# The first loads and the first two head pairs of a tree-masked attention kernel, put in another order

## The chip, the cores and the metric

One core of one Trainium2 chip runs the kernel. The metric is the device time of one execution in microseconds (us); the time before is 132.62 us, the median of three runs (132.22 to 132.91). Engines are named as in the profile: PE is TensorE (PEld its weight loads), DVE VectorE, ACT ScalarE, POOL GpSimd, SP SyncE.

## The reference

Attention over 8 batches of 12 heads (96 heads in all), 512 positions of 64 numbers. A position may see itself and its ancestors in a binary tree, in which the parent of i is (i-1)//2.

```python
for i in range(seq):
    mask[i, i] = 1
    parent = i
    while parent > 0:
        parent = (parent - 1) // 2
        mask[i, parent] = 1
scores = np.einsum('bhqd,bhkd->bhqk', Q, K) * scale
scores = scores + (1 - mask) * (-1e9)
weights = np.exp(scores - np.max(scores, axis=-1, keepdims=True))
weights = weights / (np.sum(weights, axis=-1, keepdims=True) + 1e-10)
return np.einsum('bhqk,bhkd->bhqd', weights, V).astype(np.float32)
```

Inputs and output are float32.

## The kernel before

**Pairs.** The 96 heads are worked on as 48 pairs, `i` from 0 to 47. A pair passes through these steps, each of them a function of the program:

- `transpose(i)` (steps "T", or "K" and "Q" for the two halves alone): TensorE turns K and Q of the pair, so that the 64 numbers lie across partitions, into one PSUM tile `kqp`. There is a single buffer for it (the pool `psT` has one), so the transposes of a pair wait until VectorE has copied those of the pair before.
- `evac(i)`: VectorE copies `kqp` to the SBUF tile `kq` (L459 in the first four pairs).
- `scores1(i)` and `scores2(i)` (step "S"): TensorE multiplies mask codes (L503, L528) and keys and queries (L508, L534) into the PSUM tiles `s1` and `s2`; ScalarE takes the exponentials (L519, L550) into `e`.
- `values(i - 1)` and `norm(i - 1)` (step "V"): TensorE multiplies exponentials and `vt` into `ob` (L561); `vt` is V in the order of the tree, with a column of ones that gives the sums. VectorE takes the reciprocal of the sums (L594) and multiplies (L599).

**V copies.** V is loaded as `vst` and brought into the order of the tree by small copies, `spread` (L309), each named by (block of 16 heads, part 0 to 9, first head, last head). Which engine makes which copy, and behind which pair, is written out in the tables `BY_VECTOR` and `BY_SCALAR`; the rest is GpSimd's. Step "D" issues VectorE's copies of the pair's number, step "A" ScalarE's; where a string has no "D" or "A", they come at its end.

**Order.** Nothing is scheduled by a tool: each engine runs its instructions in the order in which the program issues them. For the first six pairs the order of the steps is a string in the list `FIRST`; later pairs use "STV" and the like. Step "X" is `spin`: two matmuls of zeros on TensorE (L745) that nobody reads. Ahead of the loop stand nine more of these, the cast of the first loads (L758), and the transposes and evacuation of pair 0.

**Loads.** K and Q of heads 0 and 1 come through the queues of SP and ACT into `ol`, as float32. All other loads, and nearly all stores, are issued by GpSimd in one program, the list `ops`, and cast to bf16 on the way; `load_k`, `load_q` and `load_v` take the first head and the number of heads (L260; L270 for the groups from head 8 on). Between the loads stand GpSimd's own copies: `eye_order` and `code_order` (the tiles `mixed`, L243, and `qcoarse`, L248) early on. An operation of `ops` is issued as soon as the pairs are far enough (`ready`), and then runs in the order of the list.

Of the kernel before, what the change touches and what calls it, by code (L numbers as in the profile page):

```python
# [124 lines left out]
def kernel(  # L125
# [495 lines left out]
    def pool_program():  # L621

        K_BEFORE = {
            6: (load_k, 8 * KB, KB), 10: (spread_top, 5, 0, KB), 11: (store, nc.gpsimd, 5),
        }

        Q_BEFORE = {
            3: (load_k, 5 * KB, KB), 4: (load_k, 6 * KB, KB), 5: (spread_top, 3, 0, KB), 6: (spread_top, 3, KB, VB),
            9: (spread_top, 4, KB, VB), 10: (spread_top, 5, KB, VB),
        }  # L630
        ops = [
            (load_k, 2, 2), (load_q, 2, 2), (load_v, 0, 8), (load_k, 4, 4),
            (load_q, 4, 2), (load_q, 6, 2), (load_k, 8, 8), (load_q, 8, 8), (eye_order,),
            (load_v, 8, 8), (code_order, 0), (code_order, 64),
            (load_k, 16, 8), (load_q, 16, 8), (load_v, 16, 8),
            (load_k, 24, 8), (load_q, 24, 8), (load_v, 24, 8),
            (load_k, 32, 8), (spread_top, 0, KB, VB), (spread_top, 1, 0, KB),
            (load_v, 32, 8), (load_q, 32, 8), (load_k, 40, 8),
            (spread_top, 1, KB, VB),
        ]  # L640
        stored = 0
        for h in range(40, NH, KB):
            if h == 40:
                ops += [(load_v, h, KB), (load_q, h, KB)]
            else:
                ops += [(load_k, h, KB), (load_q, h, KB)]
            if h + KB < NH:
                ops.append((load_v, h + KB, KB))
            if h % VB == KB:
                ops.append((spread_top, h // VB, 0, KB))  # L650
            elif h >= 48:
                ops.append((spread_top, h // VB - 1, KB, VB))
            while KB * stored + KB + BEHIND <= h + KB:
                ops.append((store, nc.gpsimd, stored))
                stored += 1
        ops.append((spread_top, NH // VB - 1, KB, VB))
        ops += [(store, nc.gpsimd, q) for q in range(stored, NH // KB - 1)]
        ops += [(store_pair, nc.gpsimd, i) for i in (NP - 4, NP - 3)]
        for g in BESIDE["Q"]:
            if g in Q_BEFORE:  # L660
                ops.insert(ops.index(Q_BEFORE[g]), (lay_q, g))
                continue
            at = ops.index((load_q, KB * g, KB)) + 1
            behind = 0
            while behind < LANES:
                behind += {load_k: 1, load_q: 1, load_v: 1, store: 2, store_pair: 1}.get(ops[at][0], 0)
                at += 1
            ops.insert(at, (lay_q, g))
        for g in K_BY_POOL:
            before = K_BEFORE.get(g, (lay_q, g))  # L670
            ops.insert(ops.index(before), (lay_early, g))
        return ops

    def ready(op, i):
# [16 lines left out]
        return i >= GP * (args[1] + 1)  # L691

    BY_VECTOR = {
# [29 lines left out]
    def spread_by(copy, table, steady, i):  # L723
# [6 lines left out]
        for args in todo:  # L730
            spread(copy, *args)

    program = pool_program()

    def pool(i):
# [22 lines left out]
        nc.vector.tensor_copy(out=kept[0][:, 0:2, :, :], in_=first[src][:, :, :, :])  # L758
    TWICE = (9,)
    K_TURN = {3: 7, 4: 10, 5: 14}  # L760
    FIRST = ['XKSQ', 'SXXXKXQDVAT', 'SVATT', 'SVTT', 'STV', 'STVD']
    done = 1
    pool(-1)
    transpose(0)
# [2 lines left out]
    for i in range(NP + 1):  # L767
        steps = FIRST[i] if i < len(FIRST) else "STVT" if i in TWICE else "SVT" if i == 8 else "STV"
        for n, step in enumerate(steps):
# [67 lines left out]
```

## Time and profile before

| | before |
|---|---|
| time, median of 3 runs | 132.62 us |
| time of the profiled execution | 132.39 us |
| its span | 130.6 us |
| busy: PE, DVE, ACT, POOL | 114.5, 96.8, 97.9, 95.5 us |
| read and written in HBM | 37.86 MB, 12.58 MB |

The span runs from the first to the last recorded event of the execution; the time includes what lies around it. Times within the trace are us from the span's start. A row of the timeline gives start, duration, engine, line of the kernel, operation, output tile <- input tile with their shapes, the number of instructions, and in brackets how long the engine sat idle before and what ended that. A row of the chain of waits gives start, duration and the work that the end depended on at that moment. "To landing" of a load is the time from its issue until its data are there.

### The profile page before, as it was taken

The numbers are of one execution on the slowest core, as the hardware profiler recorded it, in microseconds if no ns is written. First come the engines' busy times: TensorE is split into PE (matmuls) and PEld (weight loads), VectorE is DVE, ScalarE is ACT, GpSimd is POOL, SyncE is SP. The second block draws the span as 40 slices with busy tenths as digits, with TensorE's granted clock in tenths as the row PEclk, the third lists the DMA queues.
The fourth block names the chain that finished last, engine by engine and source line by source line (L and its number), as shares of the span: only waits on it lengthen the run. The fifth ranks groups of instructions, "written<-read, shape, count | busy, mean of one in ns | idle before, by whom it ended". The sixth has DMA issues, their size and how long they took to land.

```text
span 130.6 us, 4946 instructions
## 1 busy us (share of the span) xinstructions
PE 114.5 (88%) x2130; PEld 82.2 (63%) x2131; DVE 96.8 (74%) x185; ACT 97.9 (75%) x160; POOL 95.5 (73%) x147
## 2 busy tenths in 40 slices
PE   4989767899799878699999999999999999989960
PEld 1343545667576656477676777776777768766640
DVE  4529957774996897996996877898958788666560
ACT  4359245797766695868979789789798997898940
POOL 6999546029779899999999999669899999200420
PEclk9999999999999999999999999999999999999995
DMA  2999999999999999999999999999999999999993
GB/s 86 228 185 205 214 198 215 195 211 205 208 201 210 206 208 201 211 203 211 206 207 207 209 347 226 203 336 241 204 311 266 267 382 385 379 388 403 380 355 136
DMA packets 24533, 32.12 MB, mean 246 GB/s; under 512 B 945, under 2 KB 15921, under 8 KB 24513
## 3 DMA queue, kind: packets, MB, share of 16 engines
q0 software_dynamic: 23232, 30.67, 111.0%
q1 hardware_dynamic: 720, 0.70, 1.6%
q10 hardware_dynamic: 560, 0.46, 1.1%
q8 instruction: 16, 0.26, 0.7%
q14 instruction: 5, 0.03, 0.1%
HBM read 37.86 MB, written 12.58 MB: 386 GB/s over the span
## 4 chain that ended last, share of the span: by engine, by line
PE 48%; DVE 25%; ACT 12%; DMA 5%; issue 5%; POOL 1%; ACTq 0%; POOLq 0%
PE ob L561 14%; DVE vt L309 7%; DVE of L599 6%; ACT e L550 6%; PE s L503 6%; PE kqp L384 6%; PE s L528 6%; DVE kq L445 6%; DMA vst<-in_V_dram 5%; PE kqp L406 5%; PE s L534 5%; PE s L508 5%; ACT e L519 4%; DVE kq L453 2%; DVE rec L594 2%
## 5 line engine op out<-in xcount | busy, mean ns | idle before, releaser
L519 ACT ACTIVATE e<-s 128x1024 bf16<-128x1024 f32 x48 | 49.2, 1024 | 23.2 <-PE s L508 22.6
L309 POOL COPY vt<-vst 32x256 uint32<-32x256 uint32 (+2 forms) x70 | 35.9, 512 | 10.7 <-DMA vst<-in_V_dram 7.6
L550 ACT ACTIVATE e<-s 128x384 bf16<-128x384 f32 (+1 forms) x92 | 41.4, 504 | 0.0
L561 PE MATMUL ob<-vt,e 128*128 128x65 bf16 (+1 forms) x940 | 37.3, 197 | 2.5 <-DVE of L599 1.8
L561 PEld LDWEIGHTS <-e 128*128 128x128 bf16 (+1 forms) x960 | 31.4, 102 | 7.8 <-DVE of L599 3.2
L599 DVE TENSOR_TENSOR of<-ob,rec 128x512 f32<-128x512 f32 x44 | 30.4, 692 | 1.5
L309 DVE COPY vt<-vst 32x512 uint32<-32x512 uint32 (+4 forms) x37 | 20.4, 552 | 1.7 <-DMA vst<-in_V_dram 0.7
L534 PEld LDWEIGHTS <-kq 64*128 64x128 bf16 x384 | 16.3, 110 | 6.2
L508 PE MATMUL s<-kq 64*128 64x512 bf16 x96 | 18.4, 378 | 1.3 <-DVE kq L445 1.3
L594 DVE RECIPROCAL rec<-ob 128x8 f32<-128x8 f32 x47 | 9.6, 204 | 13.1 <-PE ob L561 12.9
L453 DVE COPY kq<-kqp 128x1024 bf16<-128x1024 bf16 x22 | 15.1, 688 | 3.9 <-PE kqp L384 3.3
L534 PE MATMUL s<-kq 64*128 64x160 bf16 (+1 forms) x384 | 17.9, 210 | 0.0
L528 PE MATMUL s<-qcoarse,codes 40*128 40x480 bf16 x88 | 16.3, 364 | 1.3 <-ACT e L550 1.1
L503 PE MATMUL s<-qcoarse,codes 40*128 40x512 bf16 x88 | 17.2, 385 | 0.0
L445 DVE COPY kq<-kqp 128x2048 bf16<-128x2048 bf16 x11 | 13.5, 1225 | 5.0 <-PE kqp L406 4.9
L607 POOL DMA_DIRECT2D out_dram<-of x11 | 9.9, 906 | 9.0 <-DVE of L599 9.0
L528 PEld LDWEIGHTS <-codes 40*128 40x128 bf16 x96 | 7.5, 95 | 11.1 <-issue 4.7
L384 PE MATMUL kqp<-mixed,Kbeside 128*128 128x128 bf16 x144 | 11.1, 220 | 1.4 <-DVE Kbeside L333 1.2
L406 PE MATMUL kqp<-ptile,Qbeside 128*128 128x128 bf16 x144 | 11.1, 220 | 0.4 <-DVE kq L453 0.4
L333 POOL COPY Qbeside<-qst 128x1024 uint32<-128x1024 uint32 x9 | 9.5, 1059 | 2.4 <-DMA qst<-in_Q_dram 2.3
L260 POOL DMA_DIRECT2D vst<-in_V_dram x12 | 10.9, 909 | 0.0
L270 POOL DMA_DIRECT2D kst<-in_K_dram x11 | 7.8, 709 | 3.4 <-PE kqp L384 1.8
(45 smaller groups left out, 100.3 us busy)
## 6 DMA issues: line engine op xcount, KB each, us to landing
out_dram<-of POOLq DMA_DIRECT2D x11, 1024.0 KB, 10.2
vst<-in_V_dram POOLq DMA_DIRECT2D x12, 512.0 KB, 14.5
kst<-in_K_dram POOLq DMA_DIRECT2D x11, 512.0 KB, 11.9
qst<-in_Q_dram POOLq DMA_DIRECT2D x11, 512.0 KB, 13.7
out_dram<-ol POOLq DMA_DIRECT2D x2, 256.0 KB, 4.2
qst<-in_Q_dram POOLq DMA_DIRECT2D x3, 128.0 KB, 7.3
ol<-in_K_dram SPq DMA_DIRECT2D x1, 256.0 KB, 3.3
ol<-in_Q_dram ACTq DMA_DIRECT2D x1, 256.0 KB, 3.9
```

The costliest lines, as they stand in the source:

```text
L309: return copy(out=dst, in_=src)
L384: nc.tensor.transpose(out=dst, in_=src, identity=perm)
L445: return nc.vector.tensor_copy(out=dst, in_=src) if x == 3 else None
L453: return nc.vector.tensor_copy(out=dst, in_=src)
L503: nc.tensor.matmul(out=columns(g, sp[:, a, :], 0, 512), lhsT=k1code[64 * a:64 * a + CODE_ROWS, :], rhs=query_codes(i, a, 0, 0, 512), start ...
L508: nc.tensor.matmul(out=columns(g, sp[:, a, :], 0, 512), lhsT=keys(i, a, TOP), rhs=queries(i, a, 0, 512), start=False, stop=True,)
L519: nc.scalar.activation(out=dst, in_=src, func=AF.Exp, scale=scale)
L528: nc.tensor.matmul(out=columns(g, flat[:, a, :], 32, 512), lhsT=k2code[64 * a:64 * a + CODE_ROWS, :], rhs=query_codes(i, a, 1, 32, 512), s ...
L534: nc.tensor.matmul(out=columns(g, flat[:, a, :], lo, hi), lhsT=keys(i, a, TILE2[t]), rhs=queries(i, a, lo, hi), start=False, stop=t == 1,)
L550: nc.scalar.activation(out=dst, in_=src, func=AF.Exp, scale=scale)
L561: nc.tensor.matmul(out=ob[lo:hi, a, 65 * t:65 * t + 65], lhsT=e[:, a, PLACE[t], lo:hi], rhs=vt[:, head(i, a) % VB, tile_v, 0:D + 1], **flags,)
L599: nc.vector.tensor_tensor(out=dst, in0=o4[:, a:a + n, :, 0:D], in1=rec[:, a:a + n, :, :].to_broadcast([P, n, 4, D]), op=ALU.mult,)
```

## The change

Three things are put in another order; no instruction of the computation is added or taken away.

- In GpSimd's program V of heads 0 to 7 is issued first, and K and Q of heads 2 and 3 (pair 1) behind it.
- Of the seven V copies that VectorE makes in the first turn of the loop, four stay there and three go to the second turn.
- The strings of the first two turns change. In the first, the scores of pair 0 come ahead of pair 1's transposes, and the V copies of VectorE and ScalarE between the two. In the second, VectorE's other V copies are issued right behind the scores of pair 1, ahead of pair 2's transposes. Of the idle matmuls (two for each "X") the first turn has three pairs instead of one, the second one pair instead of four; in all two fewer, with their weight loads.

```diff
         ops = [
-            (load_k, 2, 2), (load_q, 2, 2), (load_v, 0, 8), (load_k, 4, 4),
+            (load_v, 0, 8), (load_k, 2, 2), (load_q, 2, 2), (load_k, 4, 4),
             (load_q, 4, 2), (load_q, 6, 2), (load_k, 8, 8), (load_q, 8, 8), (eye_order,),
...
     BY_VECTOR = {
-        0: [(0, 0, 0, 8), (0, 7, 0, 8), (0, 2, 0, 8), (0, 6, 0, 8), (0, 9, 0, 4), (0, 3, 0, 8), (0, 8, 4, 8)],
-        1: [(0, 4, 4, 8)],
+        0: [(0, 0, 0, 8), (0, 7, 0, 8), (0, 2, 0, 8), (0, 6, 0, 8)],
+        1: [(0, 9, 0, 4), (0, 3, 0, 8), (0, 8, 4, 8), (0, 4, 4, 8)],
         2: [(0, 1, 4, 8)],
...
-    FIRST = ['XKSQ', 'SXXXKXQDVAT', 'SVATT', 'SVTT', 'STV', 'STVD']
+    FIRST = ['XSDAXKXQ', 'SDKXQVT', 'SVATT', 'SVTT', 'STV', 'STVD']
```

## The prediction, made before the changed kernel ran

> **What bounds the kernel now.** I read the page first. All times are microseconds from the span's start.
>
> ```profile
> span 130.6 us, 4946 instructions
> ...
> DMA  2999999999999999999999999999999999999993
> ...
> PE 48%; DVE 25%; ACT 12%; DMA 5%; issue 5%; POOL 1%; ACTq 0%; POOLq 0%
> ```
>
> The DMA engines are at nine tenths or more in every slice but the first and last. Busy alone does not say that they set the end, so I followed the chain of waits.
>
> ```profile
> 1.26 0.84 POOL kst L260
> 2.10 0.72 POOL qst L260
> 2.82 7.02 DMA vst<-in_V_dram
> 9.86 0.54 DVE vt L309
> ...
> 13.89 0.70 DVE kq L459
> 14.63 0.64 PE kqp L359 x16
> ```
>
> The chain starts with GpSimd issuing K and Q of heads 2 and 3, then V of heads 0 to 7, and waits 7.02 for that V. VectorE then runs seven V copies, 9.86 to 13.86, and only behind them evacuates pair 2's transposes (13.89), which releases pair 3's (14.63). These 7.02 are the whole 5% that DMA has of the chain. TensorE is nearly full from there on; one stretch of ten microseconds (busy of PE, PEld, DVE, ACT, POOL, then granted clock, DMA share, GB/s):
>
> ```profile
> 60.00:70.00 10.00, 9.70 (x183) 7.09 (x180) 9.11 (x17) 8.46 (x15) 9.70 (x15) 1.00 1.23 207
> ```
>
> So a gain in the head is carried along as a shift, unless the end is held by something else; the tail is looked at below.
>
> **The loads.** The view by tile gives issue to landing: in turn K of heads 2 and 3, their Q, the V, and K of heads 4 to 7, whose issue row is the last.
>
> ```profile
> DMA to landing us min/median/max: 4.2/4.2/4.2
> ...
> DMA to landing us min/median/max: 4.1/4.1/4.1
> ...
> DMA to landing us min/median/max: 7.0/7.0/7.0
> ...
> DMA to landing us min/median/max: 7.5/7.5/7.5
> ...
> 3.70 0.78 POOL L260 DMA_DIRECT2D kst<-in_K_dram  x1
> ```
>
> K lands at 1.26+4.2 = 5.5, Q at 2.10+4.1 = 6.2, V at 9.84, the next K at 11.2: in order of issue, and back to back. The change swaps order inside the first three. V is issued at 1.26; with the same 7.02 it lands at 8.28. Worked from the other end: a load of this Q's size costs 6.2-5.5 = 0.7, and two fewer stand ahead of V, 9.84-1.4 = 8.4; by V's own pace (3.64 for four times the size, so 1.8 for the two) it is 8.0. I take 8.3. Bounds: 8.0, and 9.84 if order at issue does not decide. The same bytes have moved when the third load is in, so Q of heads 2 and 3 now lands near 9.84 and K near 9.1, against 6.2 and 5.5. This is the price of the change, and the old cover was the long wait for V. Three issues in another order end at the same 3.70, so K of heads 4 to 7, and what is queued behind it, lands as before. The waits this adds: TensorE's K transposes of pair 1 now wait until 9.1 and its Q transposes until 9.84, with pair 1's scores, and behind them ScalarE's exponentials, queued behind; VectorE's copies wait for V with pair 1's evacuation queued behind.
>
> **Scores of pair 0** lose the eight K transposes that stood in front; they start some 0.3 earlier, worth nothing, since ScalarE ends its two exponentials of pair 0 before its V copies can matter:
>
> ```profile
> 9.86 1.78 ACT L309 COPY vt<-vst 32x128 uint32<-32x128 uint32 x4 [0.43 <-DMA vst<-in_V_dram]
> ```
>
> These four copies start some 0.8 earlier and end before pair 1's scores are there.
>
> **VectorE.** Its eight V copies of the head, in order (the eighth is the row at 14.61), and one late copy made with GpSimd resting:
>
> ```profile
> 9.86 0.54 DVE L309 COPY vt<-vst 32x512 uint32<-32x512 uint32 x1 [0.71 <-DMA vst<-in_V_dram]
> 10.41 0.64 DVE L309 COPY vt<-vst 32x256 uint32<-32x256 uint32 x1
> 11.06 0.78 DVE L309 COPY vt<-vst 32x512 uint32<-32x512 uint32 x1
> 11.85 0.43 DVE L309 COPY vt<-vst 32x256 uint32<-32x256 uint32 x1
> 12.30 0.22 DVE L309 COPY vt<-vst 32x128 uint32<-32x128 uint32 x1
> 12.55 0.62 DVE L309 COPY vt<-vst 32x512 uint32<-32x512 uint32 x1
> 13.20 0.66 DVE L309 COPY vt<-vst 32x128 uint32<-32x128 uint32 x1
> 14.61 0.29 DVE L309 COPY vt<-vst 64x256 uint32<-64x256 uint32 x1
> ...
> 112.02 0.42 DVE L309 COPY vt<-vst 32x512 uint32<-32x512 uint32 x1
> ```
>
> The first four now stand ahead of pair 1's evacuation, the other four behind it and ahead of pair 2's. Four copies took 9.86 to 12.28, 2.42; from 8.3 they end at 10.74. Pair 1's Q, landing at 9.84, is transposed by 10.3, so the evacuation (0.70, the chain's row) is released by the copies: 10.75 to 11.46. Behind it 0.22+0.62+0.66+0.29 and gaps of 0.1 end at 13.36. What stretches copies is GpSimd's work at the time:
>
> ```profile
> 7.94 0.96 POOL L260 DMA_DIRECT2D vst<-in_V_dram  x1
> ...
> 8.83 2.72 POOL L248 COPY qcoarse<-codes 40x512 bf16<-40x512 bf16 x4
> ...
> 12.90 0.91 POOL L260 DMA_DIRECT2D vst<-in_V_dram  x1
> ```
>
> Copies of 512 took 0.42 at rest but 0.54 and 0.78 beside qcoarse; one of 128 took 0.22, and 0.66 beside the V issue at 12.90. The first batch now lies wholly beside the issue at 7.94 and the qcoarse copies. Bounds for the four: at rest 0.42+0.42+0.29+0.29 = 1.4; with 0.66-0.22 = 0.44 more on each, 3.2. I keep 2.42: two of them had this neighbour before.
>
> The Trainium skill, page "SBUF — State Buffer", section on the two separate sides, says that VectorE in a two-port mode and GpSimd exclude each other for a whole instruction. If each of the four waited out a whole qcoarse copy (2.72/4 = 0.68), they would need 1.4+2.7 = 4.1; the rows at 10.41 and 11.06 show about 0.35 more each, so the trace agrees that they get in each other's way, though not by a whole instruction each.
>
> **TensorE behind pair 1.** Starts of its groups before:
>
> ```profile
> 7.29 0.38 PE L508 MATMUL s<-kq 64*128 64x512 bf16 x2
> ...
> 8.00 0.41 PE L359 MATMUL kqp<-ptile,qst 128*64 128x128 bf16 x8
> ...
> 11.83 0.41 PE L359 MATMUL kqp<-ptile,kst 128*64 128x128 bf16 x8
> ...
> 12.18 0.60 PE L745 MATMUL ob<-idle 128*128 128x512 bf16 x2
> ...
> 12.71 0.41 PE L359 MATMUL kqp<-ptile,qst 128*64 128x128 bf16 x8
> ...
> 13.06 0.83 PE L561 MATMUL ob<-vt,e 128*128 128x65 bf16 x20
> ```
>
> From pair 1's evacuation to pair 2's the new order holds scores of pair 1 (7.29 to 8.00: 0.71), K transposes (11.83 to 12.18: 0.35), two idle matmuls (0.53), Q transposes (0.41), with two hand-overs of 0.05: 2.10. Pair 2's evacuation thus starts at 11.46+2.10 = 13.56, not 13.89: 0.33 earlier, and VectorE's second batch (13.36) is hidden by 0.2. Without that cover it costs what it overruns. The values of pair 0 (0.83 on TensorE, from about 13.5) end at 14.35, against the evacuation's end of 14.26, so pair 3's transposes start at 14.35 instead of 14.63. Two idle matmuls fewer in all change nothing, TensorE waits there. I take 0.3 for the head. Its ends: with V at 8.0 and copies at rest, Q's landing rules (9.84+0.46, evacuation to 11.0), 0.8 earlier; with V at 8.4 and copies of 3.2, evacuation to 12.3, 0.5 later.
>
> **The tail.** The last store is issued at 127.44:
>
> ```profile
> 126.00:127.00 1.00, 0.17 (x4) 0.06 (x4) 0.83 (x5) 0.00 (x0) 0.00 (x0) 1.00 0.78 311
> ...
> 128.00:129.00 1.00, 0.00 (x0) 0.00 (x0) 0.00 (x0) 0.00 (x0) 0.00 (x0) 0.50 0.61 212
> ...
> 127.44 0.35 ACTq L616 DMA_DIRECT2D out_dram<-ol  x1
> ```
>
> The DMA engines have 0.22 unused from 126 and 0.39 from 128, and the bytes stay the same: stores ready 0.3 earlier find room, but a gain much over 0.6 would meet stores still queued. The sum: the profiled execution took 132.39 for a span of 130.6; less 0.3 gives 132.1. It lies 0.23 under the median of the runs, 132.62; put on the median the same shift gives 132.3, and that is the forecast.
>
> **Rivals.** *The whole head comes through*: V near 8.0, copies close to rest, 0.8 earlier, of which the tail passes on some 0.7: 131.9. For it, VectorE's copies at rest are short; against it, qcoarse stands exactly there.
>
> *V copies hold pair 1 back* (slower): pair 1 was evacuated before V landed, now behind four copies. From the point where those copies end after 11.1, later than before: 11.1+0.7+2.1 = 13.9. With 0.44 more on each of four, 0.5 is lost; the same in the second batch (0.22+0.42+0.22+0.29 and 4 times 0.44, 2.9 behind 12.3) puts pair 2's evacuation at 15.2, a loss of 1.3. Mean price 0.8: 133.4. By the lock rule of the Trainium skill page above, 4.1 for the first batch would give 8.3+4.1+0.7+2.1 = 15.2, the same 1.3.
>
> *The change does not do what it says*: V lands at 9.84 though issued first. Then four copies to 12.28, evacuation to 13.0, pair 2 at 15.1: 1.2 lost, 133.8. Against it, the landings kept the order of issue.
>
> *TensorE's clock drops.* Between the scores of pair 0 (to about 7.5) and of pair 1 (11.5) TensorE would have two idle pairs, K and Q: 0.53+0.53+0.41+0.41 = 1.9 in 4.0. Before, the emptiest stretch of that length among those I read holds 2.22 in 3.40 (PE busy, granted clock, DMA share, GB/s), and by the groups of the first 16 us the idle matmuls ran slower at the start than later (busy, mean ns):
>
> ```profile
> 16.80:20.20 3.40, 2.22 (x58) 1.00 1.35 203
> ```
>
> ```profile
> L745 PE MATMUL s<-idle 128*128 128x512 bf16 x9 | 3.5, 559 | 1.9 <-DVE warm L217 1.9
> ...
> L745 PE MATMUL ob<-idle 128*128 128x512 bf16 x9 | 2.8, 380 | 0.3 <-issue 0.2
> ```
>
> At 559/380, 1.47 times, over some 3.4 of matmuls, 1.6 is lost and 0.3 of it gained back: 133.9. Against it, no gap is longer than about 0.9. The Trainium skill, "TensorE: Matmul & The Clock Gate", section on why this matters, asks for gaps under about 3 us, so by it the clock stays; its section on PE-mode transposes says these do not count as busy in the same way, which speaks for the rival. No run shown here tells.
>
> **How the numbers follow.** Forecast 0.52, the whole head 0.16, copies hold pair 1 back 0.18, V no earlier 0.06, clock 0.08. A measurement tells about 0.5% from no change, 0.66 of 132.62, so 131.96 and 133.28 are the lines. The forecast's own range, 131.8 to 132.9 (the runs shown spread 0.7), is nearly all inside: I give 0.04 to faster and 0.03 to slower. Of the whole head 0.13 is faster; of the three slow cases 0.24 is slower (copies 0.12, V 0.05, clock 0.07). Faster 0.17, within 0.56, slower 0.27. The range 131.4 to 133.5 leaves out about 0.04 below and 0.15 above.
>
> **What would show it.** V's landing at 8.3 with the first V copy right behind it; Q of heads 2 and 3 near 9.8; pair 1's evacuation at 10.75 released by VectorE's own queue, not by TensorE; pair 2's at 13.56; pair 3's transposes at 14.35; the rest shifted by a like amount, and the DMA's dip at 126 filled. It is wrong if V lands after 8.8, if four copies take over 2.8, if idle matmuls or transposes lengthen around 11, or if pair 3 is 0.3 earlier and the end is not.

## The result, and the profile after

| | before | changed |
|---|---|---|
| median of 14 runs each, side by side | 132.6 us | 135.03 us |
| lowest to highest | 132.13 to 134.76 | 133.3 to 136.6 |
| ratio, changed to before | | 1.0112, 95% interval 1.0079 to 1.0146 |
| the profiled execution | 132.39 us | 136.59 us |

The kernel became slower; the median lies 1.5 us above the upper end of the forecast's range, 133.5. The ratio leaves out runs more than 1.5% above the fastest of their kernel, of the changed kernel six of the eight whose mean clock was 0.970 or less, so it states less than the medians do. The clock is part of the effect: the five runs at 0.985 or more have a median of 134.27 us, the eight at 0.970 or less one of 135.77. The profile shown is of the second longest of the 14 executions.

Two lines of the page of the changed kernel, the second the granted clock of TensorE in 40 slices of 3.4 us, in tenths:

```profile
span 134.8 us, 4942 instructions
...
PEclk9999559999999999999999999999999999999996
```

The clock stands at half in two slices, from about 13 to 20 us. The chain of waits of the changed kernel, its head (start, duration, work):

```profile
1.26 9.07 DMA vst<-in_V_dram
10.35 0.41 DVE vt L309
...
13.07 0.61 DVE kq L459
...
18.34 0.85 PE kqp L359 x15
```

As before, the chain starts with V of heads 0 to 7. It is issued at 1.26 and now first, yet its wait is 9.07 and not 7.02, and it lands later than before (10.32 against 9.84). The timeline of the changed kernel from there:

```profile
10.35 2.73 DVE L309 COPY vt<-vst 32x512 uint32<-32x512 uint32 x4 [2.93 <-DMA vst<-in_V_dram]
10.61 0.89 POOL L260 DMA_DIRECT2D vst<-in_V_dram  x1 [2.61 <-DMA vst<-in_V_dram]
11.09 0.41 PE L359 MATMUL kqp<-ptile,kst 128*64 128x128 bf16 x8 [2.28 <-DMA kst<-in_K_dram]
11.97 0.41 PE L359 MATMUL kqp<-ptile,qst 128*64 128x128 bf16 x8
13.00 0.67 DVE L459 COPY kq<-kqp 128x1024 bf16<-128x1024 bf16 x1
17.26 0.69 DVE L459 COPY kq<-kqp 128x1024 bf16<-128x1024 bf16 x1 [1.98 <-PE kqp L359]
18.16 0.62 PE L359 MATMUL kqp<-ptile,kst 128*64 128x128 bf16 x8
```

Read downwards: VectorE's four copies wait for V; pair 1's K is transposed only at 11.09, since it lands late too; pair 1's evacuation (13.00) stands right behind the copies, as forecast; then pair 2's (17.26) waits for TensorE, whose path from 13.67 on takes 3.59. Pair 3's transposes start at 18.16, against 14.63. That is 3.53 of the 4.2 by which the span grew (134.8 against 130.6).

Why the path takes 3.59 the view by windows shows (PE busy with its instructions, clock, DMA share, GB/s):

```profile
9.76:13.17 3.41, 1.47 (x19) 1.00 1.33 194
13.17:16.58 3.41, 2.85 (x24) 0.50 1.13 211
16.58:20.00 3.42, 3.42 (x51) 0.50 1.34 200
```

In one window TensorE was busy 1.47 of 3.41; the two that follow run at half clock. The Trainium skill, "TensorE: Matmul & The Clock Gate", section on what is actually happening, describes a clock decided in free-running windows of 3413 ns; by it a stretch of half clock lasts a multiple of that, and the trace agrees (6.83 here, 3.41 in another run below). The changes of the clock in each trace also show where its windows lie: here it falls at 13.17 and, at the end of the kernel, at 132.64, 35 windows later. All windows below are laid by such a change in the same trace.

Where did 3.81, the difference to the forecast 14.35 for pair 3, come from? The columns are the prediction's own steps.

| step | forecast | measured | difference |
|---|---|---|---|
| first V copy starts | 8.3 | 10.35 | +2.05 |
| four copies, to pair 1's evacuation | 2.45 | 2.65 | +0.20 |
| that evacuation | 0.71 | 0.67 | -0.04 |
| its end to pair 2's evacuation | 2.10 | 3.59 | +1.49 |
| from there to pair 3's transposes | 0.79 | 0.90 | +0.11 |

Two terms make nearly all of it, V's landing and the clock. The experiments had to tell which of them costs what, and why V lands late.

### The profile page after: what moved, and what is told of

Same layout as the page of the kernel before. It is cut to its first block, busy times and chain, and to the rows that moved or that the text cites. A ratio compares the mean times of both kernels' runs of the same rounds, so it can differ in the third digit from the quotient of the medians.

```text
span 134.8 us, 4942 instructions
## 1 busy us (share of the span) xinstructions
PE 117.0 (87%) x2128; PEld 83.1 (62%) x2129; DVE 97.6 (72%) x185; ACT 97.9 (73%) x160; POOL 95.0 (70%) x147
## 4 chain that ended last, share of the span: by engine, by line
PE 54%; DVE 23%; ACT 9%; DMA 7%; issue 4%; ACTq 0%; POOLq 0%
PE ob L561 16%; DMA vst<-in_V_dram 7%; PE s L503 7%; PE kqp L384 6%; PE s L528 6%; DVE of L599 6%; DVE vt L309 5%; PE s L508 5%; PE s L534 5%; PE kqp L406 5%; ACT e L550 5%; DVE kq L445 5%; ACT e L519 4%; DVE kq L453 2%; DVE Kbeside L333 2%
## 5 line engine op out<-in xcount | busy, mean ns | idle before, releaser
L508 PE MATMUL s<-kq 64*128 64x512 bf16 x96 | 18.9, 388 | 2.3 <-DVE kq L445 1.3
L453 DVE COPY kq<-kqp 128x1024 bf16<-128x1024 bf16 x22 | 15.1, 687 | 3.7 <-PE kqp L384 3.3
L445 DVE COPY kq<-kqp 128x2048 bf16<-128x2048 bf16 x11 | 13.5, 1225 | 5.3 <-PE kqp L406 5.1
L406 PE MATMUL kqp<-ptile,Qbeside 128*128 128x128 bf16 x144 | 11.1, 220 | 0.0
```

Source lines behind the costliest of these rows:

```text
L406: nc.tensor.transpose(out=dst, in_=src, identity=eye[:, 0:128])
L445: return nc.vector.tensor_copy(out=dst, in_=src) if x == 3 else None
L508: nc.tensor.matmul(out=columns(g, sp[:, a, :], 0, 512), lhsT=keys(i, a, TOP), rhs=queries(i, a, 0, 512), start=False, stop=True,)
```

## The experiments

"T3" is the start of pair 3's transposes in the profile, "V" the time at which V of heads 0 to 7 (or its last part) has landed.

**The changed kernel again, the load order alone, and two cures.** Four kernels on one chip (before there: 132.84). The first is unchanged.

> The changed kernel once more, for a second profile. In its first profile V of heads 0 to 7 landed 9.07 us after its issue (10.33 us), and the granted clock was half from about 13 to 20 us. Theory A (the late V does it): V lands after 9.5 us again, and the profile is over 1 us longer than that of before even where the clock stays full. Theory B (the clock does it): where the clock stays full, the time is within 0.5 us of that of before (132.6), wherever V lands.

Measured: 135.18 us, ratio 1.0198 [1.0137, 1.0258]; V at 9.27, T3 at 17.11. Timeline, then windows, of this kernel's profile:

```profile
9.30 2.72 DVE L309 COPY vt<-vst 32x512 uint32<-32x512 uint32 x4 [2.37 <-DMA vst<-in_V_dram]
11.95 0.67 DVE L459 COPY kq<-kqp 128x1024 bf16<-128x1024 bf16 x1
```

```profile
8.65:12.06 3.41, 1.47 (x19) 1.00 1.41 198
```

The same copies (2.72), the same emptiness (1.47), then half clock, though V came a whole microsecond sooner than in the first profile. Theory B falls short: the one run of four with a high clock, 0.991, took 134.27 us, 1.4 over before. The second takes the new loads back and keeps the new steps:

```diff
-            (load_v, 0, 8), (load_k, 2, 2), (load_q, 2, 2), (load_k, 4, 4),
+            (load_k, 2, 2), (load_q, 2, 2), (load_v, 0, 8), (load_k, 4, 4),
```

> The new order of steps and of V copies alone; the loads are issued as before the change (K and Q of heads 2 and 3, then V). Theory A1 (the steps do not fit, whatever the loads do): V lands at 9.8 as before, four copies, pair 1's evacuation at 12.3, 1.2 us lost in the head, about 133.8 us, the same as the changed kernel with a full clock. Theory A2 (the order of the loads makes DMA late): 132.6 to 133.2 us, as the K loads behind V land as before the change. Theory B (clock): idle time of TensorE stays about the same, so runs above 135 us appear here too.

Measured: 135.44 us, 1.023 [1.0155, 1.0304]; T3 17.92. The steps alone are as slow. But V landed at 11.16 in its profile, later than in any other, and the clock fell as well. The four copies took 1.65, since GpSimd's `qcoarse` copies, which lie beside them elsewhere, ended at 11.37, just behind their start:

```profile
11.19 1.65 DVE L309 COPY vt<-vst 32x512 uint32<-32x512 uint32 x4 [4.33 <-DMA vst<-in_V_dram]
```

```profile
8.51:11.92 3.41, 1.13 (x15) 1.00 1.39 201
```

So it did not part the two terms; the same kernel with the clock held comes below. The third adds idle matmuls to the changed kernel, to take the clock out:

```diff
-    FIRST = ['XSDAXKXQ', 'SDKXQVT', 'SVATT', 'SVTT', 'STV', 'STVD']
+    FIRST = ['XSDAXXXXXKXQXX', 'SDKXQVT', 'SVATT', 'SVTT', 'STV', 'STVD']
```

> The changed kernel with four more pairs of idle matmuls while TensorE waits for pair 1's K, and two more pairs behind pair 1's transposes; the loads and copies are the same. Theory B: the granted clock stays full in every run (0.985 or more), and runs above 135 us are gone; median 133.3 to 134.2 us. Rival: the half clock does not come from the waiting, runs above 135 us stay. With theory A the time stays above that of before by over 0.7 us even with a full clock.

Measured: 134.78 us, 1.0175 [1.0128, 1.0223]. Windows, then timeline:

```profile
9.20:12.61 3.41, 3.10 (x26) 1.00 1.38 201
```

```profile
10.26 2.74 DVE L309 COPY vt<-vst 32x512 uint32<-32x512 uint32 x4 [3.08 <-DMA vst<-in_V_dram]
...
16.53 0.41 PE L359 MATMUL kqp<-ptile,kst 128*64 128x128 bf16 x8
```

With 3.10 busy in the window the clock held through the head (0.985 to 0.997 in its runs), and T3 came at 16.53, not 18.16. Yet the time is above the 133.3 to 134.2 expected, and only 0.4 us under that of the unchanged kernel beside it. So most of the loss is there with a whole clock. With V, though, the loads behind it are late too (below); this run does not part the two. The fourth puts V second, behind K of heads 2 and 3:

```diff
-            (load_v, 0, 8), (load_k, 2, 2), (load_q, 2, 2), (load_k, 4, 4),
+            (load_k, 2, 2), (load_v, 0, 8), (load_q, 2, 2), (load_k, 4, 4),
```

> The changed kernel with V as the second load: K of heads 2 and 3, V, Q of heads 2 and 3. GpSimd's ninth load, which reuses the semaphore of the first and waited 2.6 us for V, then waits for K of heads 2 and 3. If that wait matters: 0.5 to 1 us faster than the changed kernel with a full clock. If only V's landing matters: V lands near 9.1 us (behind one small load) and the time moves by less than 0.5 us, in step with V's landing.

Measured: 135.02, 135.13, 132.37 and 134.88 us, too far apart for a ratio. V landed at 8.62, earlier than as the first load, and T3 came at 15.34. The profile, by windows, is of the first of these:

```profile
9.71:13.12 3.41, 1.87 (x31) 1.00 1.29 207
13.12:16.53 3.41, 3.41 (x48) 0.50 1.14 206
```

1.87 busy did not hold the clock. It fell a second time at 57.49 in this profile, behind a window that again has 1.87 busy; what made that one thin was not followed.

**Why V first lands late.** A load is spread over sixteen DMA engines, and the landing is that of the last. The trace has one completion for each; sorted, for V of heads 0 to 7:

```
before              8.51 8.62 8.64 8.85 8.86 8.87 8.89 8.99 9.02 9.10 9.25 9.26 9.43 9.51 9.61  9.84
changed             6.99 7.14 7.22 7.26 7.31 7.40 7.50 7.51 7.52 7.53 7.62 8.97 9.20 9.49 9.67 10.32
changed, again      7.12 7.17 7.20 7.24 7.42 7.42 7.47 7.48 7.64 7.68 7.69 8.41 8.47 8.54 8.59  9.27
more idle matmuls   7.11 7.15 7.18 7.26 7.39 7.43 7.51 7.51 7.67 7.90 8.60 8.80 8.83 8.84 9.52 10.24
steps alone         8.45 8.56 8.58 8.60 8.61 8.62 8.65 8.67 8.70 8.71 8.73 8.79 8.85 8.87 10.20 11.16
V second            7.84 7.86 7.89 7.91 7.92 7.94 8.08 8.09 8.11 8.29 8.30 8.51 8.54 8.56 8.59  8.62
```

Where V is the first load, ten or eleven engines are done by 7.9, sooner than forecast, and five or six finish 0.7 to 2.7 later. The lag does not close: the eighth load of the changed kernel has eleven completions from 16.70 to 17.23 and five from 18.02 to 19.35. So K, Q and what follows land late as well (K of heads 2 and 3 at 11.04, of 4 to 7 at 13.03). V second has no such group; in "steps alone" two engines are late although V is the third load, so it is not bound to the first place. As the third load V landed at 9.84, 9.83, 9.30, 10.52, 10.36, 10.10, 9.94 and 11.16 in the eight profiles of this document that have it there: one profile does not fix the landing to better than about a microsecond, and V first and whole (9.27 to 10.32) gained nothing over that place. The Trainium skill, "DMA: Bandwidth & Descriptors", section on why a DMA increments its semaphore by 16, says that the engines finish independently and that only the full count means landed; these lines agree.

**Before, edited.** Four kernels on another chip, compared with the kernel before there (132.96 us). The first is before itself:

> The kernel before once more, for a second profile. In the profiles so far V of heads 0 to 7 landed at 9.84 us (before), 10.32, 9.27, 10.24 (V first), 11.16 (old order of loads, new steps) and 8.62 us (V second). If V's landing varies by itself from run to run, it lies anywhere from 8.6 to 11 us here; if the old steps keep it at 9.8, the new steps have a part in it. The granted clock should stay full, ratio 1.00.

Measured: 133.15 us, 1.0009 [0.9963, 1.0055]; V 9.83, T3 14.85. This is the mark for T3 below. It is not sharp: T3 is 14.63 in the first profile of before, 15.11 and 14.74 in two kernels below that leave the V copies and pair 2 as they are. Next, the scores of pair 0 ahead of pair 1's transposes, in before, with one pair of idle matmuls more between them:

```diff
-    FIRST = ['XKSQ', 'SXXXKXQDVAT', 'SVATT', 'SVTT', 'STV', 'STVD']
+    FIRST = ['XSKXQ', 'SXXXKXQDVAT', 'SVATT', 'SVTT', 'STV', 'STVD']
```

> The kernel before with one step moved: the scores of pair 0 ahead of pair 1's K transposes. Loads, V copies and pair 1's place ahead of the V copies stay as before. Theory (the loss is pair 1 behind the V copies and the half clock): no change, ratio 0.995 to 1.005, full clock, pair 1's evacuation near 8.5 us. Rival (moving the scores is what empties TensorE and lowers the clock): a half clock shows and the time rises by over 1 us.

Measured: 132.83 us, 1.0005 [0.9973, 1.0037]. The scores' new place is free. Next, V second as above, with idle matmuls to hold the clock:

```diff
-    FIRST = ['XSDAXKXQ', 'SDKXQVT', 'SVATT', 'SVTT', 'STV', 'STVD']
+    FIRST = ['XSDAKXXQXXX', 'SDKXQVT', 'SVATT', 'SVTT', 'STV', 'STVD']
```

> The changed kernel with V as the second load and with more idle matmuls: pair 1's K transposes at once, two pairs of idle matmuls until Q lands, three more behind pair 1's transposes. Both losses named so far are addressed: the clock should stay full (0.985), V land near 8.7 us, pair 1's evacuation start at 11.1, pair 2's near 13.9 as in the kernel before. Theory: 132.3 to 133.2 us, within 0.5% of before. If it stays over 133.8 us, something else costs, and the order of the copies on VectorE is next.

Measured: 132.88 us, 0.9996 [0.9956, 1.0036]; T3 14.90. Timeline, then windows:

```profile
8.94 2.50 DVE L309 COPY vt<-vst 32x512 uint32<-32x512 uint32 x4 [1.88 <-DMA vst<-in_V_dram]
11.36 0.67 DVE L459 COPY kq<-kqp 128x1024 bf16<-128x1024 bf16 x1
14.16 0.69 DVE L459 COPY kq<-kqp 128x1024 bf16<-128x1024 bf16 x1 [0.51 <-PE kqp L359]
```

```profile
8.92:12.33 3.41, 3.04 (x21) 1.00 1.37 203
```

With V at 8.91 and the clock whole, the loss is gone. The path of TensorE, from 12.03 to 14.16, takes 2.13: the prediction's 2.10, where the clock holds. The last of the four leaves before's loads alone and moves two of VectorE's copies, one from ahead of pair 2's evacuation and one from behind it, to the third turn, where a third stood already:

```diff
-        0: [(0, 0, 0, 8), (0, 7, 0, 8), (0, 2, 0, 8), (0, 6, 0, 8), (0, 9, 0, 4), (0, 3, 0, 8), (0, 8, 4, 8)],
-        1: [(0, 4, 4, 8)],
-        2: [(0, 1, 4, 8)],
+        0: [(0, 0, 0, 8), (0, 7, 0, 8), (0, 2, 0, 8), (0, 6, 0, 8), (0, 9, 0, 4), (0, 3, 0, 8)],
+        2: [(0, 8, 4, 8), (0, 4, 4, 8), (0, 1, 4, 8)],
...
-    FIRST = ['XKSQ', 'SXXXKXQDVAT', 'SVATT', 'SVTT', 'STV', 'STVD']
+    FIRST = ['XKSQ', 'SXXXKXQVAT', 'SVATDT', 'SVTT', 'STV', 'STVD']
```

> The kernel before, with loads and steps as they were, and three of VectorE's small V copies (needed only for pair 2's values) moved from before and behind pair 2's evacuation to the third turn of the loop. Pair 2's evacuation should start at 13.2 instead of 13.89 us and pair 3's transposes at 13.95 instead of 14.63. If a shift of the head is carried to the end (prediction): 0.4 to 0.7 us faster. If the stores in the DMA queues hold the end: within 0.2 us of before.

Measured: 132.59 us, 0.9982 [0.9946, 1.0017]. No difference that these runs can tell.

```profile
14.11 0.69 DVE L459 COPY kq<-kqp 128x1024 bf16<-128x1024 bf16 x1 [0.79 <-PE kqp L359]
```

The lead that was to be tested did not come in its profile: V landed at 10.52, pair 2's evacuation waited for TensorE until 14.11, and T3 is 14.85, the mark. So this run says nothing on whether a lead is carried.

**V in two loads, and single prices.** Four more on a third chip (before there 133.34 us). V first, but as two loads of four heads, with the idle matmuls of the third experiment:

```diff
-            (load_v, 0, 8), (load_k, 2, 2), (load_q, 2, 2), (load_k, 4, 4),
+            (load_v, 0, 4), (load_v, 4, 4), (load_k, 2, 2), (load_q, 2, 2), (load_k, 4, 4),
...
-    FIRST = ['XSDAXKXQ', 'SDKXQVT', 'SVATT', 'SVTT', 'STV', 'STVD']
+    FIRST = ['XSDAXXXXXKXQXX', 'SDKXQVT', 'SVATT', 'SVTT', 'STV', 'STVD']
```

> V first and the clock held by idle matmuls, as in the run with more idle matmuls (134.78 us, V landed at 10.24), but V is two loads of four heads. With V first as one load, five or six of the sixteen DMA engines finished V a good microsecond behind the others, in three profiles of three; with V second none did. Theory 1 (the size of the first load does it): the second half lands near 8.5 us, the time falls by over 1 us, to 133.0 to 133.6. Theory 2 (V ahead of the small K and Q does it, in whatever pieces): V is whole after 9.5 us and the time stays at 134.3 or more.

Measured: 134.84 us, 1.0128 [1.0058, 1.0198]; V 8.61, T3 16.65. V lands early, and the gain is not there:

```profile
8.09 2.98 PE L745 MATMUL ob<-idle 128*128 128x512 bf16 x9
11.21 0.41 PE L359 MATMUL kqp<-ptile,kst 128*64 128x128 bf16 x8
12.55 0.69 DVE L459 COPY kq<-kqp 128x1024 bf16<-128x1024 bf16 x1 [1.20 <-PE kqp L359]
```

My own cure did this. The idle matmuls, written for a late V, ran from 8.09 to 11.1 in TensorE's order, and pair 1's K, landed at 9.28, was transposed behind them. The evacuation now waits for TensorE (1.20). The profiled execution, 136.12 us, also lost its clock at 57.30, behind a window with 1.97 busy; the other three, with clocks of 0.988 to 0.997, took 134.5 to 135.0. The experiment is repeated with fewer below. Next, two copies ahead of pair 1 instead of four, with V second and the clock held:

```diff
+        0: [(0, 0, 0, 8), (0, 7, 0, 8)],
+        1: [(0, 2, 0, 8), (0, 6, 0, 8), (0, 9, 0, 4), (0, 3, 0, 8)],
+        2: [(0, 8, 4, 8), (0, 4, 4, 8), (0, 1, 4, 8)],
...
+    FIRST = ['XSDAKXXQXX', 'SDKXQVT', 'SVATDT', 'SVTT', 'STV', 'STVD']
```

> V second and the clock held, as in the run that equalled the kernel before; but only two V copies stand ahead of pair 1's evacuation, four behind it, and the three that only pair 2's values need go to the third turn. Pair 1's evacuation should start at 10.2 to 10.5 instead of 11.36 us, pair 2's at 13.1 to 13.5 instead of 14.16, pair 3's transposes at 13.9 to 14.2 instead of 14.90. If the head's gain is carried to the end: 0.5 to 0.9 us faster than before, 131.9 to 132.4. If the stores hold the end: within 0.3 us of before.

Measured: 133.13 us, 0.9983 [0.9948, 1.0017], with T3 at 14.47, later than expected: 0.38 ahead of the mark, but only 0.16 ahead of the earliest T3 of before. A small lead at best, and no time that these runs can tell. Next, the price of the clock alone: before without its idle matmuls in the first two turns.

```diff
-    FIRST = ['XKSQ', 'SXXXKXQDVAT', 'SVATT', 'SVTT', 'STV', 'STVD']
+    FIRST = ['KSQ', 'SKQDVAT', 'SVATT', 'SVTT', 'STV', 'STVD']
```

> The kernel before without the five pairs of idle matmuls of its first two turns (the nine ahead of the loop stay); loads, copies and the order of all else are untouched. If a stretch of 3.4 us with TensorE busy for under some 1.9 us lowers the clock: a half clock shows between 10 and 20 us, and the time rises by 1 to 2.5 us, with V landing as before. Rival (the half clock comes from elsewhere): full clock, time within 0.3 us of before.

Measured: 133.74 us, 1.0051 [1.0012, 1.009]. A line of its page, one of its windows, then one of its timeline:

```profile
PEclk9999559999999999999999999999999999999995
```

```profile
9.64:13.05 3.41, 2.17 (x34) 1.00 1.32 204
```

```profile
11.73 0.41 PE L359 MATMUL kqp<-ptile,kst 128*64 128x128 bf16 x8 [0.97 <-DMA kst<-in_K_dram]
```

The same two slices at half clock as in the changed kernel, for half a per cent, less than the 1 to 2.5 us expected. The condition of that forecast, under some 1.9 busy, is not met: the clock fell behind 2.17. The longest gap of TensorE in that window is the 0.97 in which pair 2's K transposes wait for their load; in before, idle matmuls fill that time. Last, GpSimd. In the changed kernel the load of V of heads 8 to 15 is issued at 10.61 instead of 7.94: it uses the semaphore of the first load again and waits 2.61 for V (the row in the timeline above), which the prediction had not seen. Before, with that load moved behind the copies that it held up in the changed kernel:

```diff
-            (load_v, 8, 8), (code_order, 0), (code_order, 64),
+            (code_order, 0), (code_order, 64), (load_v, 8, 8),
```

> The kernel before with GpSimd's load of V of heads 8 to 15 behind its code copies, so issued at about 10.6 instead of 7.9 us, as late as the changed kernel issues it (10.61) where it waits for the first V's semaphore. If that wait is part of the loss: 0.3 to 1 us slower. If the DMA queues hold enough work at that time: within 0.2 us of before.

Measured: 133.28 us, 1.0001 [0.9966, 1.0036]:

```profile
10.46 0.91 POOL L260 DMA_DIRECT2D vst<-in_V_dram  x1
```

Issued as late as in the changed kernel, that load costs nothing by itself.

**The two cures together and apart.** Three kernels on a fourth chip (before there 132.87 us). V in two loads first, as above, with as many idle matmuls as an early V needs:

```diff
-    FIRST = ['XSDAXKXQ', 'SDKXQVT', 'SVATT', 'SVTT', 'STV', 'STVD']
+    FIRST = ['XSDAXXKXQXX', 'SDKXQVT', 'SVATT', 'SVTT', 'STV', 'STVD']
```

> V first as two loads of four heads, idle matmuls only where TensorE waits anyway (in the run before they held back pair 1's transposes, 11.21 though K had landed at 9.28). Theory: the second half of V lands near 8.6 us again with no group of late DMA engines, four copies end at 11.3, pair 1's evacuation starts there, pair 3's transposes at 14.8 to 15.0, and the time is within 0.7% of before (132.5 to 133.9). Rival (V ahead of K and Q costs by itself): over 134.3 us with V landed before 9 us.

Measured: 132.83 us, 0.9999 [0.9965, 1.0034]; V 7.83, clock whole.

```profile
7.93 3.83 DVE L309 COPY vt<-vst 32x512 uint32<-32x512 uint32 x4 [0.38 <-DMA vst<-in_V_dram]
11.68 0.67 DVE L459 COPY kq<-kqp 128x1024 bf16<-128x1024 bf16 x1
...
15.22 0.41 PE L359 MATMUL kqp<-ptile,kst 128*64 128x128 bf16 x8
```

Pair 1's evacuation to T3 takes 3.54 as forecast (10.75 to 14.35: 3.60). The loss is gone with the same intent: V first, the new steps, the copies ahead of pair 1. The head came out later than expected all the same, since the four copies took 3.83. The first alone took 1.74, beside GpSimd's `mixed` copies (7.81 to 8.61) and a load issue (8.47 to 9.42). V landed 1.08 sooner than in the kernel with V second and the clock held, and pair 1's evacuation started 0.32 later. Then before's loads with the new steps (the second experiment) and the clock held:

```diff
-    FIRST = ['XSDAXKXQ', 'SDKXQVT', 'SVATT', 'SVTT', 'STV', 'STVD']
+    FIRST = ['XSDAKXQXXXXX', 'SDKXQVT', 'SVATT', 'SVTT', 'STV', 'STVD']
```

> The new order of steps with the loads in the old order (135.44 us, half clock, pair 3's transposes at 17.92) and the clock held by five pairs of idle matmuls behind pair 1's transposes. Theory: V lands at 9.8 to 10.2, four copies to 12.4, pair 1's evacuation there, pair 3's transposes at 15.9 to 16.3, so 1.1 to 1.5 us slower than before: this is what pair 1 behind the V copies costs with neither the clock nor late engines. Rival: within 0.4 us of before, the clock did it all.

Measured: 133.34 us, 1.0054 [1.002, 1.0088]:

```profile
9.96 2.33 DVE L309 COPY vt<-vst 32x512 uint32<-32x512 uint32 x4 [2.72 <-DMA vst<-in_V_dram]
12.22 0.67 DVE L459 COPY kq<-kqp 128x1024 bf16<-128x1024 bf16 x1
```

Here V lands at 9.94: the rival "V no earlier" by itself. Its head was right, four copies to 12.28 and pair 2 at 15.1, measured 12.22 and 15.01; its price, 1.2, was not: 0.54%, some 0.7 us, which also lies between the theory and the rival of this experiment. T3 is 15.75, 0.9 behind the mark. Two evacuations (L445) further on in this trace, the second of them level with before's (51.81, below):

```profile
23.04 1.22 DVE L445 COPY kq<-kqp 128x2048 bf16<-128x2048 bf16 x1
...
51.80 1.22 DVE L445 COPY kq<-kqp 128x2048 bf16<-128x2048 bf16 x1
```

Then V in two loads alone, the steps as in the changed kernel:

```diff
-            (load_v, 0, 8), (load_k, 2, 2), (load_q, 2, 2), (load_k, 4, 4),
+            (load_v, 0, 4), (load_v, 4, 4), (load_k, 2, 2), (load_q, 2, 2), (load_k, 4, 4),
```

> The changed kernel with V first as two loads of four heads and nothing else: its idle matmuls as they are. Set against the run with the clock held, it shows the half clock alone. Theory: V whole near 8.6 us; TensorE is busy for some 1.5 to 1.9 of 3.4 us before pair 1's scores, so the clock goes to half in most runs, pair 3's transposes start at 15.3 to 16.5, and the time is 0.7 to 2 us over that of the run with the clock held. Rival: full clock, the same time.

Measured: 133.2 us, 1.0072 [1.0027, 1.0117]. Four of its ten runs have a clock under 0.985 and took 134.0 to 134.5 us, those at 0.989 or more 132.5 to 133.3. The profile is of one of the latter:

```profile
6.40:9.81 3.41, 3.08 (x37) 1.00 1.39 184
9.81:13.22 3.41, 2.21 (x33) 1.00 1.33 204
```

The clock held, with 2.21 in its thinnest window here. A stretch of the same length from 8.36 to 11.77 holds only 1.95, so how thin the thinnest window is depends on where the windows happen to lie. That the four slower runs lost their clock in this way is likely, but no trace of them is kept.

**Both leads together.** To see whether a shorter head can be carried to the end, V in two loads, two copies ahead of pair 1 (the tables of the experiment above) and the clock held:

```diff
+    FIRST = ['XSDAXKXQX', 'SDKXQVT', 'SVATDT', 'SVTT', 'STV', 'STVD']
```

> V first as two loads and only two V copies ahead of pair 1's evacuation (three go to the third turn); one pair of idle matmuls behind pair 1's transposes. Pair 1's evacuation should start near 10.5, released by Q's landing, pair 3's transposes at 13.9 to 14.2 (14.63 and 14.85 in the two profiles of before). If a gain of the head is carried to the end: 0.4 to 0.8 us faster than before. If the stores in the DMA queues take it up at the end: within 0.3 us of before.

Measured: 133.24 us against 133.63 for before on that chip, 0.9981 [0.9942, 1.002]; T3 13.93, 0.9 ahead. Timeline of this run:

```profile
21.09 1.22 DVE L445 COPY kq<-kqp 128x2048 bf16<-128x2048 bf16 x1
...
33.61 1.04 POOL L333 COPY Qbeside<-qst 128x1024 uint32<-128x1024 uint32 x1 [0.40 <-DMA qst<-in_Q_dram]
33.94 1.59 DVE L309 COPY vt<-vst 32x512 uint32<-32x512 uint32 x2
...
51.74 1.23 DVE L445 COPY kq<-kqp 128x2048 bf16<-128x2048 bf16 x1
```

and of before, the profile of the second chip:

```profile
22.14 1.23 DVE L445 COPY kq<-kqp 128x2048 bf16<-128x2048 bf16 x1
...
33.52 1.49 POOL L333 COPY Qbeside<-qst 128x1024 uint32<-128x1024 uint32 x1 [0.48 <-DMA qst<-in_Q_dram]
34.99 0.91 DVE L309 COPY vt<-vst 32x512 uint32<-32x512 uint32 x2
...
51.81 1.23 DVE L445 COPY kq<-kqp 128x2048 bf16<-128x2048 bf16 x1
```

VectorE's evacuations (L445) lead by 1.05 at 21, and by 0.07 at 52. GpSimd's copy of Q starts when its load lands, at 33.61 and 33.52, lead or no lead. VectorE's two V copies come 1.05 sooner and now lie beside it: 1.59 instead of 0.91. That accounts for 0.68 of the lead; the rest, to 0.07, is not followed row by row.

## Why the prediction was wrong

The forecast was 0.3 us faster with no measurable difference; it came out 2.4 us slower by the medians, 1.1% by the ratio.

**The step that failed first: V's landing.** "V is issued at 1.26; with the same 7.02 it lands at 8.28 ... I take 8.3. Bounds: 8.0, and 9.84 if order at issue does not decide." It landed at 10.32, 9.27 and 10.24 in three profiles with V first as one load, two of them outside the bounds and all past the 8.8 that was to show it wrong. The three estimates that agreed on 8.0 to 8.4 all took a load as one thing with one pace, from a head where the sixteen completions lay evenly over 1.3. "In order of issue, and back to back" fits the first eleven completions of the changed kernel (V's from 6.99 to 7.62, then K's from 7.80 to 8.67); it says nothing of the last five. V as the second load (8.62, 8.91, 9.05) or in two loads (8.61, 7.83, 8.41, 8.33) landed near the forecast. With the clock held and V whole, the loss is 1.75% (third experiment); with V in two, none (0.9999).

**"K of heads 4 to 7, and what is queued behind it, lands as before"** failed with it: 13.03 for 11.16. The same number of completions is late in every load behind that was looked at.

**The clock** was named as a rival with the right place, "1.9 in 4.0"; it had a chance of 0.08 and a counter-argument, "no gap is longer than about 0.9", which took K as landed at 9.1. With K at 11.04 the gap is 2.28 and the window holds 1.47. The argument by gaps fails of itself, too: before without its idle matmuls lost the clock with a longest gap of 0.97. The Trainium skill, "TensorE: Matmul & The Clock Gate", section on why this matters, was cited for gaps under about 3 us being safe; the trace disagrees: in three of these profiles the clock fell with longest gaps of 2.28, 1.54 and 0.97. What the runs show is that thin windows are at risk. In the heads the clock fell behind windows with 1.13, 1.47, 1.47, 1.87 and 2.17 busy, and held with 2.21, 3.04, 3.08 and 3.10. Busy time is not the whole rule, for the kernel with V in two and the clock held kept its clock in a later window with 2.04 (33.91 to 37.32). The rival's price, 1.3 net, fits the 1.49 of the table and the 1.5 between the changed kernel's low and high clocks. In before, where the head had cover, two half windows cost 0.5%, some 0.7 us, and in the third experiment the cure gave back only 0.4. The changed kernel's own runs part the 2.4 us best: at a high clock they are 1.7 above before, so the late landing, with pair 1 behind the copies, is the larger part; the eight of fourteen at a low clock lie another 1.5 higher.

**The copies** took 2.73, 2.72, 2.74, 2.57, 2.50, 2.65, 2.67 and 2.33 for the 2.42 forecast where `qcoarse` or a load issue lay beside them, and 1.65 where it ended just behind their start. But they took 3.83 with V at 7.83, outside the bounds of 1.4 and 3.2 and near the 4.1 that the prediction had worked out for copies that each wait out a whole `qcoarse` copy. So the rival of slow copies did show, in the kernel where V came earliest; it cost no time there (0.9999). (The mean of its two prices, 0.5 and 1.3, is 0.9 and not the 0.8 of the prediction.) That pair 1's evacuation stands behind VectorE's own queue was right.

**TensorE's path of 2.10** was right: 2.13 and, in the kernel with V in two and the clock held, pair 1's evacuation to T3 3.54 for 3.60.

**A wait was overlooked**, GpSimd's 2.61 for V before its ninth load, which uses the first load's semaphore again. The prediction had what is queued behind the first three loads go as before. The later issue alone cost nothing (1.0001).

**"A gain in the head is carried along as a shift"** failed as well, hidden by the rest. T3 0.9 ahead gives 0.9981 [0.9942, 1.002], and the lead was 0.07 at 52 us. A lag of that size is not surely carried either: with T3 0.9 behind, the evacuation at 23.04 is 0.9 behind before's 22.14 and the one at 51.80 level with it. That execution took 132.84 us, although the ten runs together give 1.0054. Larger lags stay: with T3 at 16.53, 1.68 behind, the same evacuation starts at 53.35, 1.54 behind, and the ratio is 1.0175; with T3 at 16.65 it is 1.0128. The prediction looked for what holds the end in the tail; as far as it was followed, it sits at 20 to 52 us, where one copy of GpSimd was seen to start with a load that landed when it did. So, judging by the last experiment, even V at 8.3 would not have made the kernel measurably faster.

**Open.** Why five or six engines are late when V is the first load and whole, three profiles of three, and two in one profile where it is third; which engines these are and what else was on them, the traces here do not tell. Also open are the exact rule of the clock, and whether the late V or the late loads behind it cost more. No version here is shown to be faster than before: 0.9981, 0.9982 and 0.9983 all have intervals that hold 1.

## What to carry to other kernels

A load lands with its slowest DMA engine: before moving a large load to the front, look at the completions of all sixteen, in more than one profile, and try it in two pieces or as second. An earlier landing can put the work behind it beside another engine's copies, as with V at 7.83. Where an edit takes work off TensorE or makes it wait, add up its busy time in stretches of 3.4 us wherever they may lie, not only the gaps. Give idle matmuls to the thin ones, but no more than the wait holds, for they stand in the queue ahead of the next real work. A change of the head by less than about 1 us may be gone before the end, so follow one row past the middle of the kernel before counting it.

## What the hardware showed unexpectedly

The same bytes, issued at the same 1.26, landed at 10.32, 9.27 and 10.24 as one load, while eleven, eleven and ten of the engines had their share by 7.9; the two halves of the same V, first again, had landed by 7.83 to 8.61. The clock fell with no gap of TensorE longer than 0.97, behind a window with 2.17 of 3.41 busy, and held with 2.21 in another kernel and 2.04 in a third. One VectorE copy of 512, 0.42 at rest, took 1.74 beside GpSimd's copies and load issue.
